# One buffer more for the first blocks' results, full scatters for the second blocks, and two weight splits moved

## The chip, the cores and the metric

The program runs on one core of a Trainium2 chip. The metric is the device time of one execution in microseconds (us). A profiled execution has its own time, some us from the median of the plain runs; spans, busy times and waits are read from that one. PE is the matmul engine (PEld its weight load), DVE the vector engine, ACT the scalar engine, POOL the engine that issues the indirect DMAs, SP the queue that issues the plain loads and stores.

## The reference

One encoder layer on 2048 tokens of 1024 numbers: a token mixer, then a mixture of 32 experts, then a norm. The change lies in the experts. Each token goes to two of them:

```python
def run_block(args):
    tok, e = args
    xb = hf[jnp.minimum(tok, n_tok - 1)]
    a = xb @ w_gate[e]
    b = xb @ w_up[e]
    return (jax.nn.silu(a) * b) @ w_down[e]
...
out = (out.reshape(n_slots, dm) * slot_gate[:, None])
y = jnp.zeros((n_tok, dm)).at[slot_tok].add(out, mode='drop')
```

The three weights of an expert are 1024x512, 1024x512 and 512x1024 floats, 6.3 MB together.

## The kernel before

The token mixer fills the first half of the span; it writes the normed tokens to `h2d` and the residual to `acc`, both in DRAM, and a table of slots. From about 830 us the experts run, in an order of places e = 0 to 31 set by how many tokens they have. Every place has a fixed capacity. Most are **narrow**: 128 rows, one block (`Block`, `core`). Thirteen are **wide** (`Wide`): places 3, 7, 11 with 224 rows, 15, 19, 23, 27 with 176, 21, 25, 29 with 160, 13 and 17 with 144, and the last, 31, with 288. So places 1 to 12 run as three narrow and one wide in each four, and from 12 on narrow and wide alternate. A wide place has a first block of 128 rows and a second block with the rest (96, 48, 32 or 16 rows).

For one place POOL gathers its rows from `h2d` (`xg`, L234); PE turns them (`pxt`, L242), multiplies by the gate and up weights (`pg`/`pu`, or `pgu` for wide), turns the gated product (`pu<-ident,act`) and multiplies by the down weights (`py`, `pyb`). DVE weighs the result into `y` (L340 narrow, L487 wide), and POOL adds the rows of `y` to `acc` by an indirect DMA with an add (L348 narrow; L492 wide, second block first). These adds follow one another: each waits until the one before it has landed.

Matmuls run on pairs of fp32r numbers: a weight is split into a high part (`ehi`, ACT, L142) and a low part (`elo`, DVE, L143). Each expert has 12 units of 128x1024 to split. While place e computes, the units of place e+1 are split: `take(n)` in `between` issues n of them at named points of place e (its start, "gate", "silu", "up0", "up1", "turn", "down", "end"). That fixes the order in which low parts stand on DVE beside the gating (`act<-act,pu`, L319), the low parts of the turned product (`al`, L327) and the weighing (`y`). Engines run their instructions in order, so what stands behind a waiting one waits too.

`y` is one buffer of 128x1024 (name "y", one of its kind). A narrow place weighs into it. A wide place uses it twice: for the sum in the gating (L432, L433) and for its first block's result. A second buffer, "yi", holds a wide place's activations and then its second block's result.

Of the kernel before, what the change touches and what calls it, by code (L numbers as in the profile page):

```python
# [8 lines left out]
F32 = mybir.dt.float32  # L9
# [9 lines left out]
P = 128  # L19
T = 2048  # L20
D = 1024
# [32 lines left out]
def body(ctx, tc, x, c, ada_w, ada_b, norm1_g, w_in, conv_w, conv_b, w_q, w_k, b_igate, b_fgate,  # L54
# [3 lines left out]
    V, S, G, PE, SP = nc.vector, nc.scalar, nc.gpsimd, nc.tensor, nc.sync  # L58
# [4 lines left out]
    acc = dram.tile([T, D], F32, name="acc")  # L63
# [19 lines left out]
    six = [const.tile([P, NE], I32, name=f"six{b}") for b in range(NB)]  # L83
# [17 lines left out]
    def wide_at(q):  # L101
        return q > 0 and rank_at[q] < len(WIDE)

    def cap_at(q):
        return WIDE[rank_at[q]] if wide_at(q) else P if q else 2 * P
# [4 lines left out]
    def indices(b, cols, pin=lambda i: i):  # L110

        tok = slots[:, b, 0, cols]
        pin(V.tensor_scalar(gix[b][:, cols], tok, float(T - 1), None, op0=OP.min))
        pin(V.tensor_copy(six[b][:, cols], tok))
# [49 lines left out]
    wb, ps = Tiles(), Banks()  # L164
# [26 lines left out]
    def keep(i):  # L191
        return tc.keep_in_program_order(i) if ps.pool else i
# [26 lines left out]
    def at_of(tiles, tile_0, e, b):  # L219

        return tiles[b][:, e:e + 1] if e or b else tile_0
# [62 lines left out]
    class Block:  # L284
# [50 lines left out]

        def weigh(self, hf):
            if self.y is None:
                self.y = wb.tile([P, D], F32, name="y", tag="y" if self.e or self.b else "xhl")
            cs = slice(hf * 512, hf * 512 + 512)
            keep(V.scalar_tensor_tensor(self.y[:, cs], self.py[hf], at_of(gts, slot_0[:, 1:2], self.e, self.b),  # L340
                                        gate_f[:, cs], op0=OP.mult, op1=OP.mult))

        def add(self):
            at = bass.IndirectOffsetOnAxis(ap=at_of(six, six_0, self.e, self.b), axis=0)
            with ExitStack() as order:
                if not (self.e or self.b):
                    order.enter_context(tc.issue_after(scats[-1].ins))
                keep(G.indirect_dma_start(out=acc[:, :], in_=self.y, in_offset=None, bounds_check=T - 1,  # L348
                                          oob_is_err=False, out_offset=at, compute_op=OP.add))

    class Wide:

# [29 lines left out]
        def begin(self):  # L382

            R = self.R
            if self.both:
                self.ya[0] = wb.tile([P, D], F32, name="y")
                self.ya[1] = wb.tile([P, D], F32, name="y", tag="yi")
                self.act = self.ya[1][:, 0:4 * R].rearrange("p (i r) -> p i r", r=R)
                self.sum = self.ya[0][:, 0:2 * R].rearrange("p (i r) -> p i r", r=R)
            else:  # L390
                t_ = hx.tile([P, 2 * D], F32, name="act", tag="h", bufs=4)
                self.act = t_[:, 0:4 * R].rearrange("p (i r) -> p i r", r=R)
# [83 lines left out]
        def weigh(self, b, hf):  # L476
            r = self.blocks[b][2]
            if b not in self.ya:
                self.ya[b] = wb.tile([P, D], F32, name="y", tag=("y", "yi", "xw")[b])
            cs = slice(hf * 512, hf * 512 + 512)  # L480
            y, p_ = self.ya[b][0:r, cs], self.py[b, hf][0:r, :]
            if len(self.parts[b]) > 2:
                at = self.parts[b][3]
                keep(S.activation(y, self.py[b, hf][at:at + r, :], AF.Copy))
                keep(V.tensor_tensor(y, p_, y, op=OP.add))  # L485
                p_ = y
            keep(V.scalar_tensor_tensor(y, p_, gts[b][0:r, self.e:self.e + 1], gate_f[0:r, cs], op0=OP.mult, op1=OP.mult))  # L487

        def add(self, b):
            r = self.blocks[b][2]  # L490
            at = (six_h if b else six[b])[0:r, self.e:self.e + 1]
            keep(G.indirect_dma_start(out=acc[:, :], in_=self.ya[b][0:r, :], in_offset=None, bounds_check=T - 1,  # L492
                                      oob_is_err=False, out_offset=bass.IndirectOffsetOnAxis(ap=at, axis=0),
                                      compute_op=OP.add))

# [1242 lines left out]
    with mctx:  # L1738
# [8 lines left out]
        cm = wb.pools[2] = mctx.enter_context(tc.tile_pool(name="cm", reuse_waits="tile", bufs=1, side="right"))  # L1747
# [4 lines left out]
        def turn_slots():  # L1752
            tb = of_order["tb"]
            tp = ps.tile([P, 2, NB * NE], F32, name="ptb", tag="pxt", bufs=2)
            for i in range(2):
                PE.transpose(tp[:, i, :], tb[:, i::2], ident[:NB * NE, :NB * NE])
            of_order["tp"] = tp

        def place_slots():
            tp = of_order["tp"].rearrange("p v (b e) -> p b v e", b=NB)  # L1760
            keep(V.tensor_copy(slots[:, :, :, dyn], tp[:, :, :, dyn]))
            indices(0, dyn, keep)

        six_h = cm.tile([P, NE], I32, name="six_h")

        def place_further():
            for b in range(1, NB):
                indices(b, dyn, keep)

            lim = wb.tile([P, NE], F32, name="lim")  # L1770
            for q in range(1, NE):
                keep(V.memset(lim[:, q:q + 1], float(cap_at(q))))
            keep(V.tensor_tensor(lim[:, dyn], cnts[:, dyn], lim[:, dyn], op=OP.is_gt))
            keep(V.scalar_tensor_tensor(six_h[:, dyn], lim[:, dyn], 2.0 * T, slots[:, 1, 0, dyn], op0=OP.mult, op1=OP.add))
# [116 lines left out]
        def take(n):  # L1891
            for _ in range(n):
                next(feed, None)

        for e in range(NE):


            nxt, turning = [], []
            last = e == NE - 1

            def between(m, e=e, nxt=nxt, turning=turning, last=last):

                wide = wide_at(e)
                if m == "gate":
                    take(2 if e else 0)
                elif last:
                    pass
                elif m == "silu":
                    take(2 if wide or not e else 1)
                elif m == "up0":  # L1910
                    take(2 if wide else 1)
                elif m == "up1":
                    take(2)
                elif m == "x":
                    if not nxt:
                        nxt.append(Wide(e + 1) if wide_at(e + 1) else [])
                        turning.append(nxt[0].turn_x() if wide_at(e + 1) else turned_x(e + 1, 0, nxt[0]))
                    for _ in range(2 if e == NE - 2 else 1):
                        next(turning[0], None)
                elif m == "turn":  # L1920
                    take(1)
                    for _ in range(2 if e else 0):
                        next(late, None)
                elif m == "down":
                    for _ in turning[0]:
                        pass
                    gather(e + 2, 0)
                    take(2 if wide or not e else 3)
                elif m == "end":
                    take(1)  # L1930
                if e == 0 and m == "silu":
                    turn_slots()
                    place_slots()
                    gather(1, 0)
                elif e == 0 and m == "up0":
                    place_further()
                if e == NE - 4 and m == "silu":
                    for _ in late:
                        pass
                    fg.append(cm.tile([P, D], F32, name="fg", tag="lle"))  # L1940
                    SP.dma_start(fg[0], row_ap(final_g, D))

            if e:
                take(2)
                gather_further(e + 1)
            if e == 0:
                core(0, 1, x1[0], between)
                gather_further(1)
            elif last:
                last_core(x0, between)  # L1950
            elif wide_at(e):
                wide_core(x0, between)
            else:
                core(e, 0, x0, between)
            x0 = nxt[0] if nxt else None
# [4 lines left out]
    with tc.If(n_late > 0):  # L1960
        with ExitStack() as lctx:
# [9 lines left out]
            with tc.For_i(0, n_late, 1) as j:  # L1971
# [14 lines left out]
                                     in_offset=bass.IndirectOffsetOnAxis(ap=gi[:, 0:1], axis=0))  # L1986
# [35 lines left out]
                y = lb.tile([P, D], F32, name="ly")  # L2022
                for hf in range(2):
                    cs = slice(hf * 512, hf * 512 + 512)
                    py = ps.tile([P, 512], F32, name="lpy")
                    for k in range(4):
# [6 lines left out]
                                     in_=y, in_offset=None, bounds_check=T - 1, oob_is_err=False,  # L2033
# [49 lines left out]
```

## Time and profile before

| | |
|---|---|
| median of 3 runs | 1692.88 us (1690.27 to 1693.51) |
| profiled execution | 1697.99 us, span 1696.1 us |
| PE busy | 1533.4 us, 90% of the span |
| DVE busy | 1372.7 us, 81% |
| ACT, POOL busy | 924.4 us, 303.0 us |

The profiled execution is 5.1 us above the median of the runs. How to read it: the share of busy time says little, since every engine is busy most of the time; what counts in the expert phase is where PE stops, what it waits for, and what that waits for in its turn. A row of the timeline gives start, length, engine, line, operation, what is written and read, how many instructions are merged, and in brackets the idle time before and what ended it.

### The profile page before, as it was taken

To read this page: it belongs to the slowest core of one execution; us is meant where nothing else is said; L and a number is where in the kernel's file an instruction comes from. 1 tells how busy PE (TensorE), PEld (TensorE's weight loads), DVE (VectorE), ACT (ScalarE), POOL (GpSimd) and SP (SyncE) were. 2 spreads that over 40 slices of the span, in tenths; PEclk is the share of its full clock that TensorE was granted. 3 is DMA by queue.
4 is the path that set the end of the run, shared out by engine and by line. 5 is a ranking of instruction groups with operands and counts; after the bars stand their busy time and mean duration, and the time that the engine had idled before them with its cause. 6 is when DMAs were issued, how large, how long until landed. Compare 5 with 4: busy or idle time off the path is not lost. (4 is left out here: it accounts for less than half of the span.)

```text
span 1696.1 us, 25252 instructions
## 1 busy us (share of the span) xinstructions
PE 1533.4 (90%) x8789; PEld 1314.9 (78%) x8789; DVE 1372.7 (81%) x2757; ACT 924.4 (55%) x1492; POOL 303.0 (18%) x165
## 2 busy tenths in 40 slices
PE   3989999998989999998899799797999999998992
PEld 3868887887978888866788688686888888887871
DVE  6889878997879879989687687876888887888847
ACT  4235545564455645556266466554666666666651
POOL 0000000011020002000232334231333322233210
PEclk9999999999999999999999899898999999999996
DMA  8973375425552345256597897877988888998865
GB/s 309 310 242 97 94 247 173 137 63 144 191 101 75 112 162 135 78 188 259 158 331 270 298 350 279 308 274 249 305 301 287 289 283 298 321 315 276 268 239 218
DMA packets 142562, 383.06 MB, mean 226 GB/s; under 512 B 16772, under 2 KB 68011, under 8 KB 126046
## 3 DMA queue, kind: packets, MB, share of 16 engines
q1 hardware_dynamic: 124374, 340.95, 58.2%
q0 software_dynamic: 13024, 38.95, 9.1%
q10 hardware_dynamic: 5032, 1.51, 0.4%
q8 instruction: 70, 1.15, 0.3%
q14 instruction: 62, 0.51, 0.1%
HBM read 338.77 MB, written 46.25 MB: 227 GB/s over the span
## 5 line engine op out<-in xcount | busy, mean ns | idle before, releaser
L143 DVE TENSOR_TENSOR elo<-eraw,ehi 128x1024 fp32r<-128x1024 f32 x384 | 451.1, 1216 | 71.3 <-ACT ehi L142 70.9
L142 ACT ACTIVATE ehi<-eraw 128x1024 fp32r<-128x1024 f32 x384 | 378.1, 1047 | 0.0
L142 ACT ACTIVATE whi<-wraw 128x1024 fp32r<-128x1024 f32 (+1 forms) x100 | 105.8, 1058 | 149.2 <-PE big L239 107.1
L239 PE MATMUL pgu<-x,ehi 128*128 128x288 f32 (+3 forms) x896 | 155.9, 325 | 9.2 <-DVE y L423 9.2
L239 PE MATMUL big<-hh,whi 128*128 128x512 f32 x384 | 158.5, 413 | 0.0
L239 PE MATMUL big<-hh,wlo 128*128 128x512 f32 x384 | 153.6, 401 | 2.0 <-DVE wlo L143 2.0
L239 PE MATMUL big<-hl,whi 128*128 128x512 f32 x384 | 154.4, 402 | 0.0
L239 PEld LDWEIGHTS pgu<-x,ehi 128*128 128x128 f32 x896 | 141.0, 190 | 12.9 <-DVE y L423 9.4
L143 DVE TENSOR_TENSOR wlo<-wraw,whi 128x1024 fp32r<-128x1024 f32 (+1 forms) x100 | 122.3, 1223 | 19.9 <-ACT whi L142 19.1
L234 POOL DMA_INDIRECT xg<-h2d,gix x47 | 71.3, 1517 | 372.2 <-PE pxt L242 294.1
L239 PE MATMUL pg<-ehi,x 128*128 128x256 f32 (+1 forms) x608 | 122.5, 351 | 1.3 <-DVE y L485 1.1
L239 PEld LDWEIGHTS pg<-ehi,x 128*128 128x128 f32 x608 | 100.6, 199 | 14.8 <-DVE y L485 1.5
L239 PE MATMUL py<-ehi,ah 128*128 128x512 f32 x256 | 109.0, 426 | 0.6 <-ACT ah L440 0.6
L239 PE MATMUL big<-whi,yl 128*128 128x512 f32 x256 | 99.1, 402 | 8.6 <-DVE yl L143 8.4
L239 PE MATMUL big<-whi,yh 128*128 128x512 f32 x256 | 104.5, 409 | 2.3 <-ACT yh L142 2.3
L239 PE MATMUL py<-ehi,al 128*128 128x512 f32 x256 | 102.3, 400 | 0.6 <-DVE al L327 0.6
L239 PE MATMUL py<-elo,ah 128*128 128x512 f32 x256 | 102.2, 399 | 0.0
L239 PE MATMUL pgu<-x,elo 128*128 128x176 f32 (+4 forms) x832 | 101.4, 275 | 0.0
L239 PE MATMUL big<-wlo,yh 128*128 128x512 f32 x256 | 101.4, 397 | 0.0
L239 PEld LDWEIGHTS pgu<-x,elo 128*128 128x128 f32 x832 | 100.7, 192 | 0.4
L1380 POOL DMA_INDIRECT table<-pay,si x28 | 35.8, 1279 | 361.7 <-DVE si L1375 211.1
L348 POOL DMA_INDIRECT acc<-y,six x20 | 66.0, 3300 | 137.3 <-DVE y L340 127.4
(462 smaller groups left out, 3485.0 us busy)
## 6 DMA issues: line engine op xcount, KB each, us to landing
eraw<-in_w_expert_gate_dram SPq DMA_DIRECT2D x64, 1024.0 KB
eraw<-in_w_expert_up_dram SPq DMA_DIRECT2D x64, 1024.0 KB
eraw<-in_w_expert_down_dram SPq DMA_DIRECT2D x128, 512.0 KB
wraw<-in_w_in_dram SPq DMA_DIRECT2D x64, 512.0 KB
adaw<-in_ada_w_dram SPq DMA_DIRECT2D x40, 512.0 KB
wraw<-in_w_out_dram SPq DMA_DIRECT2D x36, 512.0 KB
xq<-in_x_dram SPq DMA_DIRECT2D x16, 512.0 KB
bcs<-mad SPq DMA_DIRECT2D x16, 512.0 KB
```

The source lines that it names most:

```text
L142: i = S.activation(hi, src, AF.Copy)
L143: j = V.tensor_tensor(lo, src, hi.bitcast(F32), op=OP.subtract)
L234: gathers.append(keep(G.indirect_dma_start(out=xg[0:n], out_offset=None, in_=h2d[0:r, :], bounds_check=r - 1, oob_is_err=False, in_offset= ...
L239: keep(PE.matmul(*args, **kw))
L348: keep(G.indirect_dma_start(out=acc[:, :], in_=self.y, in_offset=None, bounds_check=T - 1, oob_is_err=False, out_offset=at, compute_op=OP. ...
L1380: st = G.indirect_dma_start(out=table[:, :], out_offset=bass.IndirectOffsetOnAxis(ap=si[:, i, t:t + 1], axis=0), in_=pay[:, t, i, :], in_o ...
```

## The change

- A tile "y" now has two buffers that are used in turn, for narrow places (`Block.weigh`) and for the first block of wide ones (`Wide.begin`, `Wide.weigh`).
- The second block's buffer "yi" becomes one lasting tile, cleared once by a memset before the experts with pooled buffers start; its scatter (`Wide.add`, b = 1) now names all 128 rows of it. Rows beyond the place's tokens have an index outside `acc` and are dropped.
- In narrow places the calls of `take` are dealt out anew: 1 unit at "gate" (was 2), none at "silu" (was 1), 2 at "up0" (was 1), 2 at "turn" (was 1). The sum of 12 stays.

```diff
-                self.y = wb.tile([P, D], F32, name="y", tag="y" if self.e or self.b else "xhl")
+                self.y = wb.tile([P, D], F32, name="y", bufs=2) if self.e or self.b else wb.tile([P, D], F32, name="y", tag="xhl")
...
-                self.ya[0] = wb.tile([P, D], F32, name="y")
-                self.ya[1] = wb.tile([P, D], F32, name="y", tag="yi")
+                self.ya[0] = wb.tile([P, D], F32, name="y", bufs=2)
+                self.ya[1] = beside_y[0]
...
-            r = self.blocks[b][2]
-            at = (six_h if b else six[b])[0:r, self.e:self.e + 1]
-            keep(G.indirect_dma_start(out=acc[:, :], in_=self.ya[b][0:r, :], in_offset=None, bounds_check=T - 1,
+            at = (six_h if b else six[b])[:, self.e:self.e + 1]
+            keep(G.indirect_dma_start(out=acc[:, :], in_=self.ya[b], in_offset=None, bounds_check=T - 1,
...
+        beside_y.append(cm.tile([P, D], F32, name="yi"))
+        V.memset(beside_y[0], 0.0)
...
-                    take(2 if e else 0)
+                    take((2 if wide or last else 1) if e else 0)
...
-                    take(2 if wide or not e else 1)
+                    take(2 if wide or not e else 0)
...
-                    take(2 if wide else 1)
+                    take(2 if wide or e else 1)
...
-                    take(1)
+                    take(1 if wide or not e else 2)
```

On DVE, from the weighing of narrow place 4 (`y<-py`) to that of place 5, before:

```order
L340 SCALAR_TENSOR_TENSOR y<-py_9705,slots,gate_f 128x512
L340 SCALAR_TENSOR_TENSOR y<-py_9717,slots,gate_f 128x512
L143 TENSOR_TENSOR elo<-eraw,ehi 128x1024 x5
L319 TENSOR_TENSOR act<-act,pu 128x256
L143 TENSOR_TENSOR elo<-eraw,ehi 128x1024
L327 TENSOR_TENSOR al<-pu,ah 128x256
L319 TENSOR_TENSOR act<-act,pg 128x256
L143 TENSOR_TENSOR elo<-eraw,ehi 128x1024 x2
```

And the same piece now:

```order
L340 SCALAR_TENSOR_TENSOR y<-py_9700,slots,gate_f 128x512
L340 SCALAR_TENSOR_TENSOR y<-py_9712,slots,gate_f 128x512
L143 TENSOR_TENSOR elo<-eraw,ehi 128x1024 x3
L319 TENSOR_TENSOR act<-act,pu 128x256
L143 TENSOR_TENSOR elo<-eraw,ehi 128x1024 x2
L327 TENSOR_TENSOR al<-pu,ah 128x256
L319 TENSOR_TENSOR act<-act,pg 128x256
L143 TENSOR_TENSOR elo<-eraw,ehi 128x1024 x2
```

Two of the five low parts ahead of the gating now stand behind it: one between the gating and `al`, the other further down, ahead of the next weighing (at "turn").

On POOL, around wide place 13, with the buffers' numbers (`six_h` is the second block's index, `six0` the first's), before:

```order
L234 DMA xg_11535<-h2d_58,gix1_75 16x1024
L492 DMA acc_57<-y_11222,six_h_8545 2048x1024
L492 DMA acc_57<-y_11221,six0_77 2048x1024
L234 DMA xg_11731<-h2d_58,gix0_74 128x1024
L348 DMA acc_57<-y_11751,six0_77 2048x1024
```

And now:

```order
L234 DMA xg_11534<-h2d_58,gix1_75 16x1024
L494 DMA acc_57<-yi_8546,six_h_8545 2048x1024
L494 DMA acc_57<-y_11221,six0_77 2048x1024
L234 DMA xg_11730<-h2d_58,gix0_74 128x1024
L348 DMA acc_57<-y_11750,six0_77 2048x1024
```

No DMA moves; the second block's add reads the lasting tile `yi_8546`.

## Rows read from the trace of the kernel before

**Rows 1.** Windows of places 1 to 4 and 5 to 8; columns in the first row.

```profile
core 0: us, PE busy (x) PEld busy (x) DVE busy (x) ACT busy (x) POOL busy (x), PEclk, DMA share, GB/s
862.40:949.90 87.50, 87.32 (x517) 77.42 (x516) 75.09 (x97) 57.95 (x76) 28.50 (x8) 1.00 0.90 316
949.90:1050.70 100.80, 89.83 (x517) 79.39 (x516) 77.90 (x99) 60.01 (x78) 32.87 (x10) 0.93 0.86 298
```

**Rows 2.** Waits, 860 to 1660 us: waiting operation, releaser, total us, times, longest.

```profile
PE pu L242 <- DVE act L319: 42.5, 11, 11.0
...
DVE y L340 <- DMA acc<-y,six: 35.8, 6, 11.1
...
ACT y L432 <- DMA acc<-y,six: 11.5, 8, 2.4
...
PE pgu L239 <- DVE y L423: 9.2, 1, 9.2
```

**Rows 3.** Timeline of PE at its stops; start, length, operation, idle time before.

```profile
970.60 0.69 PE L242 MATMUL pu<-ident,act 128*128 128x128 f32 x2 [10.78 <-DVE act L319]
...
1169.69 0.61 PE L239 MATMUL pgu<-x,ehi 128*128 128x288 f32 x1 [9.18 <-DVE y L423]
...
1400.82 0.44 PE L242 MATMUL pu<-ident,act 128*128 128x128 f32 x2 [2.84 <-DVE act L319]
...
1552.52 0.47 PE L242 MATMUL pu<-ident,act 128*128 128x128 f32 x1 [5.42 <-DVE act L319]
```

**Rows 4.** Timeline of DVE around the weighing of place 4.

```profile
948.90 3.48 DVE L143 TENSOR_TENSOR elo<-eraw,ehi 128x1024 fp32r<-128x1024 f32 x3
963.13 1.41 DVE L340 SCALAR_TENSOR_TENSOR y<-py,slots,gate_f 128x512 f32<-128x512 f32 x2 [10.75 <-DMA acc<-y,six]
964.46 5.76 DVE L143 TENSOR_TENSOR elo<-eraw,ehi 128x1024 fp32r<-128x1024 f32 x5
970.13 0.41 DVE L319 TENSOR_TENSOR act<-act,pu 128x256 f32<-128x256 f32 x1
```

**Rows 5.** Timeline of POOL: adds and gathers around places 3 and 13.

```profile
933.52 8.36 POOL L492 DMA_INDIRECT acc<-y,six_h  x1 [0.30 <-issue]
950.53 3.33 POOL L492 DMA_INDIRECT acc<-y,six  x1 [8.65 <-DVE elo L143]
954.16 1.06 POOL L234 DMA_INDIRECT xg<-h2d,gix  x1 [0.31 <-PE pg L239]
964.82 2.31 POOL L348 DMA_INDIRECT acc<-y,six  x1 [9.60 <-DMA xg<-h2d,gix]
...
1190.64 3.24 POOL L492 DMA_INDIRECT acc<-y,six_h  x1 [2.34 <-DVE y L487]
1197.58 6.12 POOL L492 DMA_INDIRECT acc<-y,six  x1 [3.70 <-DVE elo L143]
```

**Rows 6.** Windows right after PE's stops; columns as in rows 1.

```profile
1251.30:1255.40 4.10, 4.09 (x19) 3.70 (x20) 2.76 (x4) 2.27 (x3) 2.54 (x1) 0.58 1.03 392
...
970.60:975.50 4.90, 4.90 (x20) 4.50 (x21) 3.12 (x5) 2.27 (x3) 0.00 (x0) 0.50 1.02 339
...
1169.70:1173.40 3.70, 3.70 (x16) 3.70 (x16) 2.31 (x3) 2.60 (x4) 0.00 (x0) 0.50 1.01 238
1071.70:1074.40 2.70, 2.70 (x13) 2.70 (x14) 1.47 (x2) 1.97 (x3) 0.00 (x0) 0.50 1.03 322
1401.00:1405.50 4.50, 4.50 (x23) 4.01 (x23) 3.72 (x5) 2.62 (x4) 2.37 (x1) 0.63 0.99 378
```

**Rows 7.** Timeline of PE in place 1: gate, turn of the product, turn of the next rows.

```profile
862.35 3.79 PE L239 MATMUL pg<-ehi,x 128*128 128x512 f32 x16
...
872.11 0.38 PE L242 MATMUL pu<-ident,act 128*128 128x128 f32 x2
...
874.46 0.60 PE L242 MATMUL pxt<-ident,xg 128*128 128x128 f32 x4
```

**Rows 8.** Timeline of ACT: the sum's first use of `y` in wide place 15.

```profile
1226.59 0.47 ACT L432 ACTIVATE y<-pgu 128x352 f32<-128x352 f32 x1 [0.65 <-DMA acc<-y,six]
```

More of the change, by code (lines that the diff above doesn't have):

```diff
@@ L349, in add @@
                                           oob_is_err=False, out_offset=at, compute_op=OP.add))
+    beside_y = []
     class Wide:
@@ L478, in weigh @@
             if b not in self.ya:
-                self.ya[b] = wb.tile([P, D], F32, name="y", tag=("y", "yi", "xw")[b])
+                self.ya[b] = beside_y[0] if b == 1 else wb.tile([P, D], F32, name="y", tag="xw") if b else \
+                    wb.tile([P, D], F32, name="y", bufs=2)
             cs = slice(hf * 512, hf * 512 + 512)
```

## The prediction

> **What bounds the kernel now.** I read the windows of the expert phase first. Places 1 to 4 and places 5 to 8 do the same work, the same 517 matmul records: 87.5 us with PE busy for 87.32, then 100.8 us with PE busy for 89.83 and its clock at 0.93 [rows 1]. So PE sets the pace wherever it isn't stopped, and 13.3 us of every four places are stops and what follows them. The list of waits says what stops PE: the turn of the product waits 42.5 us, in 11 stops, for DVE's gating, and once 9.2 us for DVE's sum L423 [rows 2].
>
> Next the timelines. PE's three long stops are 10.78, 11.0 and 9.18 us [rows 2, 3]; the other nine waits for the gating add up to 42.5 - 10.78 - 11.02 = 20.7 us (the 11.02 is the 11.0 of the waits). The two largest are 2.84 and 5.42 [rows 3]. All nine lie in a narrow place right behind a wide one.
>
> A long stop, on DVE: its low parts end at 952.4, then it stands 10.75 us in front of place 4's weighing, until the add of place 3's first block has landed and `y` is free; behind it stand five low parts and then the gating that PE wants [rows 4]. POOL tells why that add lands so late: the second block's add is issued at 933.52 and holds POOL for 8.36 us, and the first block's starts only at 950.53, when the other has landed; it lands at 963.1 [rows 4, 5]. So the bound of a long stop is: two adds in series, then `y`.
>
> After each long stop PE's clock is granted at 0.50, which is its lower level, 1.2 GHz: for 4.9, 2.7 and 3.7 us of matmuls; after two of the short stops the windows show 0.58 over 4.1 us and 0.63 over 4.5 us [rows 6]. A matmul that takes twice as long gives up half of that time: (4.9 + 2.7 + 3.7)/2 = 5.65 us, and 0.42 x 4.1 + 0.37 x 4.5 = 3.4 us.
>
> **Two buffers of `y`.** Place 4 now weighs into the buffer that place 3 does not use; the last reader of it is place 2's add, some 50 us old. The six waits of DVE (35.8 us) and the eight of ACT in the sum (11.5 us) [rows 2] should go. Of DVE's and ACT's waits only PE's stops count: 10.78 + 11.02 + 9.18 = 30.98 us, with the clock 36.6.
>
> What is late next? Without the wait, DVE gets to place 4's weighing when its low parts end. In the new order two more low parts stand ahead of it; a low part takes (970.13 - 964.46)/5 = 1.134 us [rows 4]. With DVE's small waits inside place 4 filled by them I put the weighing at 953.5, not 952.4 + 2.3. Then 1.33 us of weighing and three low parts: gating at 958.2. PE wants its product 872.11 - 862.35 = 9.8 us after the gate starts [rows 7], here at 949.9 + 9.8 = 959.7. It holds with 1.1 us to spare.
>
> The next place's rows are closer. PE turns them 874.46 - 862.35 = 12.1 us after the gate starts [rows 7], for place 5 at 962.0. Their gather is issued at 954.16, behind the first block's add on POOL, and has landed when place 4's add is released, by about 964.6 [rows 5]; today the stop hides that. With four low parts instead of six behind place 3's weighing, POOL's 8.36 us should become about 6, and gather and landing come 2 us earlier at best, with the 96 rows become 128 perhaps not at all. I bound a new stop there at 0 to 6 us and take 2, in places 5 and 9: -4. At place 13 PE needs the rows later, and nothing is lost.
>
> The Trainium skill's page "SBUF — State Buffer" (section "Who interferes with whom") says that a DVE instruction with both inputs in SBUF blocks a GpSimd instruction that reads SBUF, for as long as it lasts. A low part is such an instruction. The rows bear out a part: an add of 8.36 us beside six low parts, but one of 2.31 beside five [rows 4, 5]. If the rule held strictly, the first block's add would wait at 948.5 for the end of the run of low parts, the gather would land at about 968, and the new stop would be 6 us in two places: 8 us less gain, 1651.
>
> **The low parts behind the gating.** Two low parts less ahead of the gating are 2.27 us. Seven of the nine short stops are below that and go; the two larger ones lose 2.27 each. So 20.7 - (2.84 - 2.27) - (5.42 - 2.27) = 17.0 us, and the 3.4 us of slow clock after two of those that go. The stop of 5.42 keeps 3.15 and its slow clock; other small DVE work stands there. The cover of the moved parts: one stands ahead of `al`. PE uses `al` shortly before it turns the next rows, 874.46 - 872.11 = 2.35 us after it begins to turn the product [rows 7]; `al` now comes two low parts, 2.27 us, and its own time after the gating. Where the gating ends a us ahead of the turn that is just hidden; if the cover is gone, it costs up to 0.5 us in each of 18 narrow places, 9 us, which I keep for the range.
>
> **Second blocks as 128 rows.** No more data move: the added rows are dropped. The one price is time until landing. A second add of 16 rows has landed 6.9 us after its start (1190.64 to 1197.58), one of 96 rows 17.0 us after (933.52 to 950.53), and a full add 12.6 us after (950.53 to 963.13) [rows 4, 5]. So between 0 and +10 us for each of the nine short second adds; I take +3, nearer the short ones, since the data are the same. With two buffers nobody on PE's path waits for it: price 0. The memset (a few tenths of a us to about 1) falls at about 831 us, where DVE waits for ACT; 0.
>
> **Loads.** The weights of four places, gathers and adds are 298 GB/s x 100.8 us = 30.0 MB [rows 1]. Places 1 to 4 ran without a stop at 316 GB/s, DMA 0.90 busy. Places 5 to 8 would need 30.0 MB in 88 to 90 us, 335 to 340 GB/s; they start with loads less far ahead, since today's stop lets them catch up. I charge 3 us over the three stops, bounds 0 to 10 (the first rival).
>
> **Sum.** 36.6 - 4 - 3 + 17.0 + 3.4 = 50.0 us. The profiled execution (1697.99, span 1696.1) would become 1648; it is 5.1 above the median of the runs, so the forecast for the runs is 1692.9 - 50 = 1643 us.
>
> **Rivals.**
> - *Transfers take over.* If 316 GB/s, DMA 0.90 busy [rows 1], is all that can be kept up, places 5 to 8 and 9 to 12 take 30.0/0.316 = 95 us instead of 90: with the late gather the gain falls by 10 or so, more if loads of the alternating places are late as well: 1650 to 1660. For it: DMA is already busy at 0.98 to 1.06 in the short windows [rows 6]. Against it: 378 and 392 GB/s there. Chance 0.17.
> - *The split order only moves work.* DVE has the same 12 low parts in each place. If it is late behind a wide place by its whole load, and not by what stands ahead of the gating, PE stops later by the same amount: 20.4 less, 1663. For it: DVE is 75 of 87.5 us busy and loses more to small waits [rows 1]. Against it: that leaves 12 us in four places. Chance 0.12.
> - *The long stops stay*, since something else holds the weighing back (a slot that is given out in another order, or a release that is bound to both buffers): only 17 + 3.4 are gained, 1672. Chance 0.07.
> - *Slower: the adds grow until they hold the next wide place.* From place 13 on, adds of a wide place must land before the next wide place's sum takes the same `y` buffer (L432, at 1226.59 for place 15 [rows 8]). Two full adds of 17 us in series from 1190.64 on end at 1225, just in time. If the second add of 128 rows takes beyond that, every us more stops ACT's sum and soon PE, in nine wide places; gathers behind the adds on POOL come late too. At 7 us more each, 9 x 7 = 63 us are lost against 50 gained: 1706. By the Trainium skill's page "DMA: Bandwidth & Descriptors" (section "The descriptor swizzle") a transfer of 128 partitions gives each engine 8 of them, so few valid rows would sit on few engines; no row here shows an engine's share. Chance 0.05.
>
> **Chances and range.** Forecast 0.59. A time within 0.2%, 3.4 us, cannot be told from no change by a measurement of this kernel. All cases but the last are faster by more; some of the long-stop case and of the last one fall near zero: faster 0.90, same 0.04, slower 0.06. The likeliest case reaches from 1635 (no late gather, no late load) to 1652 (gather as by the strict rule, or `al` late everywhere). With the transfers' case and the split's the range is 1633 to 1668.
>
> **What will show it.** DVE's wait L340 for `acc<-y,six` and ACT's L432 for it gone from the waits; places 5 to 8 in 88 to 92 us at clock 1.00; a stop of 0 to 6 us of PE in front of `pxt` in places 5 and 9, released by the gather; the stops behind wide places at 0 to 0.6 us, one of about 3. Low parts that wait for ACT's high parts, and those for a load, would show the transfers' case. It is wrong if PE's stops for `act` L319 stay above 15 us in total, or if L432 (then L434) still waits for an add.

## The result and the profile after

The changed kernel takes 1643.55 us (median of 4 runs, 1641.74 to 1648.86) where the kernel before takes 1693.2 in the same comparison: ratio 0.971, 95% interval 0.968 to 0.974. The forecast was 1643. The profiled execution took 1648.86 us, span 1646.8; the sum made against the profiled execution before had given 1648.

The windows of the changed kernel, cut where the first gate matmul of places 5, 9, 13, 14 and 31 begins; columns as in [rows 1]:

```profile
952.80:1044.50 91.70, 89.11 (x518) 78.61 (x517) 77.80 (x100) 59.79 (x78) 28.95 (x11) 0.98 0.92 330
1044.50:1135.30 90.80, 89.20 (x526) 78.24 (x525) 79.49 (x104) 61.26 (x81) 30.96 (x12) 1.00 0.92 332
1135.30:1161.40 26.10, 26.00 (x178) 23.07 (x177) 20.95 (x32) 16.22 (x27) 5.32 (x3) 1.00 0.95 333
1161.40:1569.30 407.90, 400.67 (x2462) 354.92 (x2461) 360.14 (x491) 270.60 (x386) 116.66 (x50) 0.99 0.86 305
```

And the same of the kernel before, places 9 to 12, 13, and 14 to 30:

```profile
1050.70:1152.50 101.80, 90.59 (x525) 79.61 (x524) 78.87 (x102) 60.63 (x80) 33.66 (x11) 0.95 0.86 299
1152.50:1189.40 36.90, 27.72 (x178) 24.84 (x177) 20.64 (x31) 16.35 (x27) 7.67 (x5) 0.86 0.72 225
1189.40:1615.50 426.10, 401.80 (x2462) 355.91 (x2461) 360.21 (x489) 270.11 (x385) 133.27 (x50) 0.99 0.84 292
```

Places 5 to 8 fall from 100.8 us to 91.7, places 9 to 12 from 101.8 to 90.8, place 13 from 36.9 to 26.1, places 14 to 30 from 426.1 to 407.9. With place 31 and the tail (80.6 to 77.5) and 0.1 in places 1 to 4 that is 52.3 us; place 1 itself began 3.0 us later in this execution (865.3 where it was 862.3), and 49.3 are left in the span.

The waits of the changed kernel from 860 to 1610 us (waiting operation, releaser, total us, times, longest) answer to [rows 2]:

```profile
DVE act L319 <- PE pu L239: 13.3, 11, 3.8
...
ACT y L434 <- PE pgu L239: 4.4, 6, 1.0
...
PE pxt L242 <- DMA xg<-h2d,gix: 3.8, 2, 2.4
...
PE pu L242 <- DVE act L319: 2.9, 2, 2.3
...
PE py L239 <- DVE al L327: 0.6, 3, 0.3
```

DVE's wait L340 and ACT's L432 (now L434) for an add are gone; PE's wait for the gating is 2.9 us where it was 42.5. Of the eleven waits two are left, and 11 times it is now DVE's gating that waits for PE's product `pu`.

PE's larger stops in the changed kernel (start, length, operation, idle time before), and the windows behind three of them:

```profile
967.41 0.38 PE L242 MATMUL pxt<-ident,xg 128*128 128x128 f32 x1 [2.38 <-DMA xg<-h2d,gix]
1058.15 0.38 PE L242 MATMUL pxt<-ident,xg 128*128 128x128 f32 x1 [1.41 <-DMA xg<-h2d,gix]
1504.42 0.48 PE L242 MATMUL pu<-ident,act 128*128 128x128 f32 x1 [2.31 <-DVE act L319]
1557.21 0.29 PE L242 MATMUL pxt<-ident,xg 32*128 32x32 f32 x1 [0.98 <-DVE x L379]
1562.73 0.48 PE L242 MATMUL pxt<-ident,xg 128*128 128x128 f32 x1 [1.79 <-DVE x L379]
```

```profile
967.40:971.70 4.30, 4.29 (x17) 3.66 (x18) 1.74 (x3) 2.23 (x4) 1.01 (x1) 0.60 1.05 313
1504.40:1507.60 3.20, 3.18 (x15) 3.18 (x16) 2.57 (x3) 2.27 (x3) 0.00 (x0) 0.50 1.04 270
1562.70:1569.00 6.30, 6.27 (x18) 4.69 (x19) 3.49 (x7) 4.25 (x7) 0.00 (x0) 0.50 0.00 0
```

The first two are the new stops in places 5 and 9, in front of the next rows and released by their gather; after the first the clock is granted at 0.60 over 4.3 us, which costs 0.40 x 4.3 = 1.7. The third, in place 28, is what is left of the 5.42 of [rows 3]. The last two, in place 30, were smaller before (1.64 together) and had no slow clock behind them.

DVE and POOL around the weighing of place 4 in the changed kernel, against [rows 4] and [rows 5]:

```profile
956.33 1.39 DVE L340 SCALAR_TENSOR_TENSOR y<-py,slots,gate_f 128x512 f32<-128x512 f32 x2
957.65 3.48 DVE L143 TENSOR_TENSOR elo<-eraw,ehi 128x1024 fp32r<-128x1024 f32 x3
961.35 0.42 DVE L319 TENSOR_TENSOR act<-act,pu 128x256 f32<-128x256 f32 x1 [0.22 <-PE pu L239]
```

```profile
936.40 6.19 POOL L494 DMA_INDIRECT acc<-yi,six_h  x1 [0.30 <-issue]
951.08 2.10 POOL L494 DMA_INDIRECT acc<-y,six  x1 [8.49 <-DVE x L261]
953.48 3.87 POOL L234 DMA_INDIRECT xg<-h2d,gix  x1 [0.30 <-issue]
```

No idle time stands in front of the weighing, and the gating waits 0.22 us for PE, not PE for it. On POOL the first block's add, at 951.08, still comes only when the second block's has landed (at 950.3 in this trace), and the gather behind it.

### The profile page after: what moved, and what is told of

It reads as the page before. It is cut to its first block, busy times and chain, and to the rows that moved or that the text cites. A ratio compares the mean times of both kernels' runs of the same rounds, so it can differ in the third digit from the quotient of the medians.

```text
span 1646.8 us, 25258 instructions
## 1 busy us (share of the span) xinstructions
PE 1531.0 (93%) x8789; PEld 1313.1 (80%) x8789; DVE 1371.1 (83%) x2758; ACT 923.0 (56%) x1492; POOL 274.8 (17%) x165
## 5 line engine op out<-in xcount | busy, mean ns | idle before, releaser
L1382 POOL DMA_INDIRECT table<-pay,si x28 | 36.9, 1319 | 366.2 <-DVE si L1377 211.1
L239 PEld LDWEIGHTS big<-hh,wlo 128*128 128x128 f32 x384 | 72.5, 189 | 18.0 <-DVE wlo L143 2.4
```

The costliest lines, as they stand in the source:

```text
L239: keep(PE.matmul(*args, **kw))
L1382: st = G.indirect_dma_start(out=table[:, :], out_offset=bass.IndirectOffsetOnAxis(ap=si[:, i, t:t + 1], axis=0), in_=pay[:, t, i, :], in_o ...
```

## The experiments

All times by place below are worked out from the start of PE's first gate matmul of each place in one profiled execution per kernel; each ratio goes by the runs of before of its own set. Places 1 to 4 took 87.4 to 87.6 us in all of them.

| kernel | ratio to before (95%) | places 5-13 | 14-30 | 31 to end |
|---|---|---|---|---|
| before | 1 | 239.5 | 426.1 | 80.6 |
| 128 rows alone | 0.9997 (0.9962-1.0032) | 238.9 | 422.8 | 79.4 |
| new order alone | 0.9867 (0.9829-0.9905) | 225.5 | 416.0 | 81.0 |
| two `y` alone | 0.9836 (0.9802-0.987) | 217.9 | 419.2 | 81.6 |
| two `y`, 128 rows | 0.9848 (0.9814-0.9883) | 217.9 | 419.1 | 78.4 |
| two `y`, new order | 0.9724 (0.9687-0.9761) | 211.3 | 406.5 | 80.7 |
| changed | 0.971 (0.968-0.9741) | 208.6 | 407.9 | 77.5 |
| changed, again | 0.9717 (0.9684-0.975) | 209.0 | 405.6 | 79.2 |
| changed, add deferred without effect | 0.9707 (0.9665-0.975) | 205.0 | 407.9 | 77.2 |
| the same, places 28 and 30 moved | 0.97 (0.9664-0.9735) | 205.0 | 405.2 | 80.6 |
| two `y`, gather ahead | 0.9735 (0.9705-0.9765) | 203.0 | 419.5 | 80.2 |
| changed, gather ahead | 0.9667 (0.9638-0.9696) | 202.7 | 406.9 | 77.9 |
| all moved | 0.9636 (0.9605-0.9667) | 202.7 | 403.5 | 75.3 |
| all moved, table spread | 0.9662 (0.964-0.9685) | 202.9 | 402.9 | 75.3 |

**The three parts one by one.** Two buffers alone:

```diff
-                self.y = wb.tile([P, D], F32, name="y", tag="y" if self.e or self.b else "xhl")
+                self.y = wb.tile([P, D], F32, name="y", bufs=2) if self.e or self.b else wb.tile([P, D], F32, name="y", tag="xhl")
...
-                self.ya[0] = wb.tile([P, D], F32, name="y")
+                self.ya[0] = wb.tile([P, D], F32, name="y", bufs=2)
...
-                self.ya[b] = wb.tile([P, D], F32, name="y", tag=("y", "yi", "xw")[b])
+                self.ya[b] = wb.tile([P, D], F32, name="y", tag=("yi", "xw")[b - 1]) if b else wb.tile([P, D], F32, name="y", bufs=2)
```

> The kernel before with two buffers of `y` alone; second blocks' adds of 96, 48, 32 or 16 rows and the old order of the low parts stay. Theory (the long stops hang on the one buffer): DVE's wait L340 for the add and ACT's L432 for it go, the three long stops with 5.65 us of half clock go, 36.6 us; the gather behind the first block's add comes late in places 5 and 9 by 2 to 6 us each, since the second block's add still stands beside six low parts; loads 0 to 3 us; the nine short stops stay at about 20 us. Time 1661 to 1672, 1666 the middle. Rival (transfers take over): gain of 15 to 20 only, 1673 to 1678, with low parts that wait for ACT and ACT for loads. Rival (something else holds the weighing): 1690 to 1696.

Measured: 0.9836, which on 1693 us is 27.8, within the 21 to 32 of the theory. The long stops are gone; the late gather takes their place at 5.37 and 4.79 us. Its windows of places 5 to 8 and 9 to 12, two of its waits, and POOL:

```profile
944.90:1040.20 95.30, 89.74 (x517) 79.14 (x516) 77.88 (x99) 60.05 (x78) 37.38 (x10) 0.96 0.90 316
1040.20:1137.00 96.80, 91.82 (x525) 80.28 (x524) 79.19 (x102) 60.67 (x80) 38.15 (x11) 0.96 0.90 314
```

```profile
PE pu L242 <- DVE act L319: 15.5, 9, 4.5
...
PE pxt L242 <- DMA xg<-h2d,gix: 10.2, 2, 5.4
```

```profile
928.51 8.35 POOL L492 DMA_INDIRECT acc<-y,six_h  x1 [0.30 <-issue]
945.37 3.46 POOL L492 DMA_INDIRECT acc<-y,six  x1 [8.51 <-DVE elo L143]
949.14 6.16 POOL L234 DMA_INDIRECT xg<-h2d,gix  x1 [0.31 <-PE pg L239]
```

Two things follow. Places 14 to 30 are 6.9 us shorter without any change of the order: the nine short stops were 20.7 us and are 15.5. And 316 GB/s with DMA 0.90 busy is here the mark of a late gather, not of a limit (below).

New order alone (the four changed calls of `take` of the change's diff, nothing else):

> The kernel before with the new order of the low parts alone (1 at gate, 0 at silu, 2 at up0, 2 at turn); one `y`, adds as before. Theory (what stands ahead of the gating decides): short stops behind wide places fall from 20.7 to about 3.7 us and two stretches of half clock go, 20.4; the long stops stay, but in places 5 and 9 three low parts instead of five stand between the weighing and the gating, 2.3 us less each, and POOL's second add beside four low parts instead of six ends about 2 us earlier, so 4 to 9 more: 1664 to 1669. Rival (the order only moves work, DVE is late by its whole load): the short stops come back behind later instructions, 1684 to 1693.

Measured: 0.9867, 22.5 us, a little under the 24 to 29 of the theory and far over the rival's 0 to 9; but less of it came where it was expected, and more elsewhere. PE's stops in places 5, 9 and 13, the largest one in a wide place (17), the one in place 28, and four waits:

```profile
963.94 0.47 PE L242 MATMUL pu<-ident,act 128*128 128x128 f32 x1 [6.54 <-DVE act L319]
1058.53 0.41 PE L242 MATMUL pu<-ident,act 128*128 128x128 f32 x1 [4.23 <-DVE act L319]
1152.89 0.61 PE L239 MATMUL pgu<-x,ehi 128*128 128x288 f32 x1 [5.39 <-DVE y L423]
...
1259.36 0.50 PE L239 MATMUL py<-ehi,ah 128*128 128x512 f32 x1 [1.93 <-ACT ah L440]
...
1525.43 0.33 PE L242 MATMUL pu<-ident,act 128*128 128x128 f32 x1 [3.23 <-DVE act L319]
```

```profile
DVE y L340 <- DMA acc<-y,six: 21.1, 6, 7.6
...
ACT y L432 <- DMA acc<-y,six: 17.5, 9, 2.8
...
PE pu L242 <- DVE act L319: 14.6, 4, 6.5
...
PE py L239 <- ACT ah L440: 4.7, 6, 1.9
```

The three long stops fall from 30.98 to 16.2 us, 14.0 us with the clock in places 5 to 13. The nine short stops do what the theory says: 20.7 us become 3.8, two stops of 0.56 (place 22) and 3.23 us (place 28). Yet places 14 to 30 gain only 10.1 us: the narrow ones among them 17.3, while the wide ones lose 7.2. The waits for the one `y` are still there, ACT's even longer (17.5 us; 11.5 in [rows 2]), and PE now waits 4.7 us for `ah`, which ACT and DVE make out of the sum in `y`; in the changed kernel, with two buffers, PE stands idle for at most 0.1 us in each of these wide places.

128 rows alone (the lasting tile and the scatter of the change's diff):

> The kernel before with the lasting buffer for second blocks, cleared once, and adds of 128 rows alone; one `y` and the old order stay. Theory (dropped rows cost little): second adds land 0 to 3 us later or a little earlier; with one `y` that moves the three long stops by as much, and ACT's L432 wait by 0 to 2 us in places from 13 on: 1688 to 1702. Rival (128 rows cost much: 7 us to landing): three long stops longer by 7 us and nine places held, 1720 or more.

Measured: 0.9997 (0.9962 to 1.0032): no change that shows, within 6 us to either side. The same from the other side, the changed kernel with the short adds again:

```diff
-            at = (six_h if b else six[b])[:, self.e:self.e + 1]
-            keep(G.indirect_dma_start(out=acc[:, :], in_=self.ya[b], in_offset=None, bounds_check=T - 1,
+            r = self.blocks[b][2]
+            at = (six_h if b else six[b])[0:r, self.e:self.e + 1]
+            keep(G.indirect_dma_start(out=acc[:, :], in_=self.ya[b][0:r, :], in_offset=None, bounds_check=T - 1,
```

> The changed kernel with second blocks' adds of 96, 48, 32 or 16 rows again, from the same lasting buffer; two buffers of `y` and the new order stay. Theory (128 rows cost nothing, since with two buffers nobody on PE's path waits for the landing): within 3 us of the changed kernel. Second adds of 16 to 48 rows land 0 to 2 us earlier than with 128. Rival (128 rows cost): 4 us or more faster. Rival (128 rows help, as the 96-row add landed after 17.0 us before and its 128 rows after 13.9 now): the stops in front of `pxt` in places 5 and 9 grow by about 3 us each, 6 to 10 us slower.

Measured: 0.9724, beside 0.9717 of the changed kernel on the same chip, so within the 3 us of the theory (1643.3 and 1641.1 us). PE's stops in front of `pxt` in places 5 and 9 were 2.51 and 2.25 us, not 3 us longer each: the rival by which 128 rows help falls too. POOL in the kernel with short adds, around place 3 (96 rows) and place 13 (16 rows), and behind it the changed kernel at place 13:

```profile
928.68 6.08 POOL L495 DMA_INDIRECT acc<-yi,six_h  x1 [0.30 <-issue]
942.83 2.63 POOL L495 DMA_INDIRECT acc<-y,six  x1 [8.07 <-DVE al L327]
...
1157.67 3.24 POOL L495 DMA_INDIRECT acc<-yi,six_h  x1 [2.34 <-DVE yi L490]
1164.53 5.06 POOL L495 DMA_INDIRECT acc<-y,six  x1 [3.62 <-DVE elo L143]
```

```profile
1162.76 3.48 POOL L494 DMA_INDIRECT acc<-yi,six_h  x1 [2.34 <-DVE yi L490]
1169.95 4.72 POOL L494 DMA_INDIRECT acc<-y,six  x1 [3.71 <-DVE elo L143]
```

From a second add's start to the start of the add behind it, which waits for the landing: 14.2 us with 96 rows, 14.7 with 128 (936.40 to 951.08); 6.9 with 16 rows, 7.2 with 128. In the old order it was 17.0 and 16.9 with 96 rows (before; two buffers alone) and 18.2 and 17.7 with 128 (128 rows alone; two `y`, 128 rows). So the length of the 17.0 of [rows 4, 5] was the old order's doing: POOL's own time for it is 8.36 beside six low parts and 6.08 to 6.19 beside four, with 96 rows as with 128.

The 128 rows do show in one place. From the end of PE's last matmul to the end of the program the six executions with 128-row adds and the work in places 28 to 31 not moved take 30.8 to 30.9 us, the five with short adds 32.2 to 32.4: the last three stores (`out_dram<-xa`) start 1.4 us earlier on POOL. Why, no run shows, and the intervals of the whole times are too wide for 1.4 us.

Two buffers and 128 rows, old order (the changed kernel without the four calls):

> The changed kernel with the old order of the low parts (two buffers of `y` and 128-row adds stay). Theory (terms add up): loses the 20.4 us of the short stops and 0 to 4 us of late gather against the changed kernel: 1664 to 1670, and within 3 us of the kernel with two buffers alone. Rival (the order only moves work): within 4 us of the changed kernel, 1640 to 1648.

Measured: 0.9848, as two buffers alone; the new order is worth 0.014, 23 us, on top of the other two.

**The changed kernel again.**

> The changed kernel itself once more, as the measure for the three beside it on the same chip: 0.968 to 0.974 of the kernel before, as in its first runs. The stops of PE should stand where they stood: in front of `pxt` in places 5 and 9 (2.38 and 1.41 us), in front of `pu` in place 28 (2.31), in front of `pxt` in place 30 (0.98 and 1.79). If the 3.0 us by which place 1 began later (1.27 already before the memset, 2.2 from a gather that landed later) are a matter of the run, they are gone or differ here; if they belong to the change, they are here again.

Measured: 0.9717. Place 1 begins at 856.3 us here, six earlier than in the execution before, so the 3.0 us were the run's. The stops in front of `pxt` were 1.16 and 2.97 us, with slow clock behind the second; those of places 28 and 30 stood as before (2.23, 0.98, 1.80).

**The late gather.** A first try deferred the add in the program:

```diff
+        if A.e in (3, 7):
+            owed.append(A)
+        else:
+            A.add(0)
-        A.add(0)
...
                     gather(e + 2, 0)
+                    if owed and owed[0].e < e:
+                        owed.pop().add(0)
```

> The changed kernel with the add of the first block of places 3 and 7 issued behind the gather that place 4 and 8 issue, not ahead of it. Theory (the two stops in front of `pxt` are a gather that stands behind an add which waits for the second block's landing): the gather is issued 1 to 3 us earlier and its packets no longer queue behind the add's; it lands by 960 instead of 967.4, both stops (2.38 and 1.41) and 1.7 us of half clock go: 4 to 6 us faster than the changed kernel. Rival (the gather is late by the low parts or by the loads, not by its place): stops of 1 us or more stay there. Rival (the add behind it lands too late for the next use of its `y`): a wait of DVE's L340 for an add appears in place 5 or 9, no gain or slower.

Measured: 0.9707 (0.9665 to 0.975). This tests nothing: the scheduler put the add back, and the order of instructions on every engine is the changed kernel's. It counts as one more run of it, with stops of 0.71 and 1.05 us in places 5 and 9 and no slow clock behind them. With the add bound to come behind the gather the order on POOL is another:

```diff
                     gather(e + 2, 0)
+                    if owed and owed[0].e < e:
+                        with tc.issue_after(gathers[-1].ins):
+                            owed.pop().add(0)
```

> The changed kernel with the add of the first block of places 3 and 7 issued behind the gather of place 6 and 10 on POOL, bound to it so that the order on POOL is really the other one (gather, add, add, where it was add, gather, add). In three runs of the changed kernel's order so far PE's stops in front of `pxt` in places 5 and 9 added up to 3.8, 4.1 and 1.8 us, with 1.7, 1.7 and 0 us of half clock. Theory (the gather stands behind an add that waits for the second block's landing, in POOL's order and in the queue): the gather is issued ahead of the landing and lands by about 958 to 960 on the scale of the changed kernel's trace (967.4 there); both stops go, 2 to 5 us faster than the changed kernel, places 5 to 12 in 177 to 179 us (182.5 and 182.8). Rival (low parts or loads make it late): a stop of 1 us or more stays. Rival (the adds now land too late): a wait of DVE for an add appears in place 5, 6, 9 or 10; no gain or slower.

Measured: 0.9667 (0.9638 to 0.9696), 0.005 or 8 us below the changed kernel's 0.9717, with intervals that still touch; 2 to 5 us had been expected. In the traces places 5 to 13 take 202.7 us, where the three executions of the other order took 208.6, 209.0 and 205.0: 2 to 6 us less. Windows of places 5 to 8 and 9 to 12, and POOL:

```profile
944.10:1031.50 87.40, 87.22 (x517) 77.42 (x516) 77.38 (x99) 59.89 (x78) 26.68 (x11) 1.00 0.94 344
1031.50:1120.70 89.20, 89.00 (x526) 78.34 (x526) 79.23 (x104) 61.47 (x81) 27.09 (x11) 1.00 0.94 338
```

```profile
927.75 6.18 POOL L494 DMA_INDIRECT acc<-yi,six_h  x1 [0.31 <-issue]
940.46 1.03 POOL L234 DMA_INDIRECT xg<-h2d,gix  x1 [6.53 <-PE pxt L242]
942.83 1.70 POOL L494 DMA_INDIRECT acc<-y,six  x1 [1.34 <-DMA acc<-yi,six_h]
```

Both stops are gone, places 5 to 12 take 176.6 us where 177 to 179 had been expected, and PE is busy for 87.22 of 87.4. The gather now waits for PE's last turn of the place's rows only, and takes POOL 1.03 us instead of 3.87.

The same edit on two buffers alone:

> The kernel before with two buffers of `y` and the gather of places 6 and 10 ahead of the first block's add; old order of the low parts, second adds with 96 to 16 rows. With two buffers alone the stops in front of `pxt` in places 5 and 9 were 5.37 and 4.79 us, with two stretches of 6.83 us at half clock, 17.0 us in all. Theory (that late gather comes from its place on POOL): both go or fall below 1 us, 12 to 17 us faster than two buffers alone, ratio to the kernel before 0.974 to 0.977 where it was 0.984. Rival (the low parts that POOL's work stands beside make it late): 0 to 5 us faster, 0.981 to 0.984.

Measured: 0.9735, 17 us faster than two buffers alone; places 5 to 13 in 203.0 us where they took 217.9. So the late gather cost 15 us there, and that is gone with its place on POOL, although the second block's add still stands beside six low parts and takes 8.34 us: the rival falls.

**What is left.** On top of the deferred add that had no effect, the table work of place 28 behind the gating and one low part of place 30 from "turn" to "down":

```diff
-                if e == NE - 4 and m == "silu":
+                if e == NE - 4 and m == "up1":
...
-                    take(1 if wide or not e else 2)
+                    take(1 if wide or e in (0, NE - 2) else 2)
...
-                    take(2 if wide or not e else 3)
+                    take(2 if wide or not e else 4 if e == NE - 2 else 3)
```

> As the kernel with the gather first, and two more moves of DVE's work: in place 28 the small DVE work on the table of further blocks (3.4 us) is issued behind the second half of the gating instead of ahead of the first, and in place 30 one of the two low parts at the point turn goes to the point down. Theory (a stop comes from what stands ahead of the instruction that PE waits for, not from DVE's load): the stop of 2.31 in place 28 with 1.7 us of half clock goes, and of the stops of 0.98 and 1.79 in place 30 with 3.4 us of half clock at least the half clock and 1 us: 8 to 9 us less than with the gather first, 12 to 15 less than the changed kernel. Rival (DVE is late by its load): the stops come back further down, 0 to 3 us less than with the gather first.

Measured: 0.97 (0.9664 to 0.9735), not told apart from 0.9717 and 0.9707; by the medians 1.4 us, which is the rival's 0 to 3 and not the 8 to 9 of the theory. Place 30 fell to 23.2 us (27.0 in the run of the unchanged order), but place 28 rose to 24.6 (23.6), with a stop of 3.5 us in front of `pxt`, and place 31 gave 3 us back. So the move in place 30 is right and that in place 28 only shifts the stop. The next kernel has the gather ahead, the move in place 30, the table work at "down", and in place 31 the work on finished rows behind the gating:

```diff
-            norm_squares(0)
             A.stage(1, 0)
             A.gated(0)
-            norm_rows(0)
-            norm_squares(4, 4)
+            norm_squares(0)
             A.stage(1, 1)
             A.gated(1)
+            norm_rows(0)
+            norm_squares(4, 4)
             norm_squares(8, 4)
```

> The changed kernel with the gather ahead as in the first of these three, and with three pieces of DVE's and ACT's work taken from in front of what PE waits for: the table work of place 28 (3.4 us) goes behind the turn of the next place's rows (point down), one low part of place 30 from turn to down, and in place 31 the squares and scalings of finished rows go behind the gating of the second half. Theory (a stop is what stands ahead of the awaited instruction): stops of 2.2 to 2.3 with 1.7 of half clock (place 28), 1 us and up to 3.4 us of half clock (place 30), and 2.4 to 3.7 with 1.7 to 3.4 of half clock (place 31) go; 3.9 + 2.7 to 4.4 + 4 to 7 less 0 to 4 us that the tail gives back since DVE's scalings end later: 8 to 14 us faster than the kernel with the gather ahead alone, ratio to the kernel before 0.959 to 0.964. Rival (DVE and ACT are full in the tail and give all of it back): 5 to 8 us only, from places 28 and 30.

Measured: 1627.8 us, 0.9636 (0.9605 to 0.9667): the lowest time of all, 5.8 us below the gather ahead by the medians (the intervals overlap) and short of the 8 to 14 expected. The sum lies in the rival's 5 to 8, but not for its reason, as the places show. Windows of places 28, 29 and 30 with the gather ahead, and with all moved:

```profile
1477.60:1500.30 22.70, 20.21 (x118) 16.92 (x117) 22.49 (x34) 14.92 (x20) 6.79 (x3) 1.00 0.91 304
1500.30:1526.90 26.60, 26.60 (x178) 24.19 (x177) 21.40 (x30) 16.51 (x27) 6.04 (x3) 1.00 0.87 312
1526.90:1553.70 26.80, 23.83 (x125) 19.83 (x124) 22.87 (x31) 17.37 (x26) 5.13 (x2) 0.87 0.64 200
```

```profile
1478.90:1498.70 19.80, 19.80 (x118) 16.96 (x118) 19.26 (x26) 15.01 (x20) 6.73 (x3) 1.00 0.88 289
1498.70:1528.60 29.90, 28.38 (x178) 25.73 (x177) 24.56 (x38) 16.43 (x27) 5.17 (x3) 0.94 0.85 313
1528.60:1551.70 23.10, 21.21 (x125) 17.92 (x124) 20.06 (x28) 14.65 (x24) 5.07 (x2) 1.00 0.75 237
```

Place 30 gains 3.7, place 31 to the end 2.6 (77.9 to 75.3); place 28 gains 2.9 and place 29 loses 3.3, so that 2.6 of the gain come from the tail, from which the rival expected nothing, and none from the move in place 28. The last run deals that table work out earlier, three pieces a place instead of two from place 8 on:

> As the kernel with all pieces moved, but the table work for further blocks is dealt out in threes instead of twos at the point turn from place 8 on, so that nothing of it is left to be done in one piece in place 28. In the kernel with all pieces moved the 3.4 us of it took the stop of 2.2 away in place 28 (19.8 us instead of 23.6) and gave one of 1.5 us with 1.7 us of half clock in place 29 (29.9 instead of 26.5), so nothing was gained by that move. Theory (a stop comes from a piece that is longer than the slack of DVE where it stands, and the slack of other places takes pieces of 0.2 to 1.2 us): places 28 and 29 together take 46.2 us or so instead of 49.7, 3 to 4 us faster, ratio to the kernel before 0.960 to 0.962. Rival (DVE is full everywhere behind place 12, and the pieces come back as stops in other places): the same time, 0.9625 to 0.965.

Measured: 1627.96 us, ratio 0.9662 (0.964 to 0.9685) to its own runs of before: the same time. Place 29 is back at 26.6, but places 14 to 27 take 333.5 us where they took 330.7, with DVE 295.94 us busy instead of 293.02:

```profile
1146.60:1480.10 333.50, 330.25 (x2045) 292.36 (x2044) 295.94 (x404) 221.41 (x316) 101.79 (x42) 1.00 0.89 313
```

The rival holds here: in places 14 to 27 DVE is busy for only 293 of 331 us, and yet 2.9 us of work more cost 2.8.

## Why the prediction was right

- **Long stops, 36.6 us: right, and shown alone.** With two buffers and the gather out of the way places 5 to 13 fall from 239.5 to 203.0, 36.5 us.
- **The late gather, 4 us (0 to 6 a place): right in place and kind, with the clock left out.** 2.38 + 1.41 + 1.7 of slow clock = 5.5 here; 5.8 (1.16 + 2.97 + 1.7) and 1.8 in the other two runs. The credit for four low parts instead of six was the larger term: with the old order 10.2 us of stops and, by the places, 15 us with the slow clock, beyond the upper bound of 12. (The 17.0 of the expectation above counts the whole of two stretches of 6.83 us at half clock, part of which fell on the stops themselves.) The add did become shorter, 8.35 to 6.19, and the gather too, 6.16 to 3.87.
- **Loads, 3 us: wrong, nothing.** With the gather ahead places 5 to 8 take 87.4 us at 344 GB/s, no more than places 1 to 4. Forecast were 335 to 340 GB/s; the first rival (316 GB/s is the limit) falls.
- **Short stops, 17.0 + 3.4: the step right, its share not the order's alone.** With the new order alone, seven stops go and two of 0.56 and 3.23 us stay; 0.57 and 3.15 were forecast. In the changed kernel places 14 to 30 gave 18.2 us. But 6.9 of that the second buffer gives by itself (nine stops of 15.5 us instead of 20.7), and with one `y` the order gains only 10.1, since ACT's and DVE's waits for `y` then stop PE in the wide places; I had put those waits at nothing. On top of two buffers the order is worth 11.3 us there (419.2 to 407.9). The order's missing share lay in the long stops and the late gather, which it shortens: 9.3 us in places 5 to 13 on top of two buffers, 14.0 by itself. That 27.8 + 22.5 comes so near to the 49 of both is therefore no proof of independent terms.
- **Place 28: forecast 3.15 us and its slow clock, measured 2.31 and 1.6 (3.2 us at 0.50). Place 30 was missed:** the low part added at "turn" stands in front of the turned rows that PE waits for; 25.0 us became 26.9 (25.5 to 27.0 in other runs).
- **`al` behind the moved parts, 0 (up to 9): 0.6 us.** The memset takes 0.91 us and nothing in the places shows it.
- **128 rows, price 0, +3 us to landing: price right, landing 0.3 to 0.5 later in the new order, about 1 in the old.** The slower rival falls: ACT's L434 waits 4.4 us for PE and for no add.
- **The strict lock rule.** The Trainium skill's page "SBUF — State Buffer" ("Who interferes with whom") speaks of a lock that is held for one instruction; that the add waits for the end of a whole run of low parts was my stricter reading of it. The add took 2.10 us beside a run of five and 3.46 with the old order; the gather's 3.87 lies beside three. By that reading the new stop was 6 us; 2.38 came (5.37 in the kernel with two buffers alone). So the trace agrees with the page in that POOL is slower beside low parts (8.36 and 6.19 us), and not with the reading that the add waits for the whole run.
- **The sum, 50.0: near the measured 49.65 in part by luck.** By places it was 36.6 - 4 - 3 = 29.6 for 5 to 13, where 30.9 came: a late gather of 5.5 to 5.9 and loads of nothing. For 14 to 30 it was 20.4, where 18.2 came. For place 31 and the tail it was nothing, where 3.1 came in this execution: 1.4 with the 128-row adds, the rest before PE's last matmul, where executions of the same order of work differ by 2 us (46.4, 46.8 and 48.4 us from the start of place 31). And place 1 began 3.0 us late. The terms erred by 1 to 3 us each, in both directions.

## What to carry to other kernels

When a wait for a buffer is removed, look for the next instruction behind the same late transfer on its queue; here it was a gather that a stop had hidden, and moving one add behind it gave another 2 to 6 us in the traces. Two edits whose gains add up need not work in the places they were meant for: run each alone and compare by stretches of the program. Where the new point of an engine's order has no slack either, moving work there only moves the stop; in place 30 it paid, since the next point had slack.

## What had not been expected

- POOL's own time for the second block's add falls by about the length of each low part that is taken away beside it: 8.36 us beside six, 6.19 beside four (2.17 for two of 1.13). A gather took 6.16 in the old order, 3.87 in the new and 1.03 where DVE's work beside it reads PSUM (`x<-pxt`, `al<-pu`). But it is no rule for every DMA: adds of 2.10 us here and 2.31 in [rows 5] have low parts beside them for nearly their whole length. What decides it, no run shows; a lock for each low part is only argued.
- Rows with an index outside `acc` cost next to nothing: 112 dropped rows added 0.3 us to the landing of an add of 16, and 32 dropped rows 0.5 to 1.3 to one of 96.
- Place 1 began between 850.2 and 865.3 us in the profiled executions, with the same order of work on PE ahead of it; single executions are better compared from there on.
